# The second half of a modulation row: products on TensorE in four groups of 32 columns in place of multiply-adds on VectorE

## The chip, the cores and the metric

The kernel runs on one core of a Trainium2 chip. The metric is the device time of one execution in microseconds, the median of several. The engines of the core run their own instruction streams in order: TensorE (PE, with its weight loads shown apart as PEld), VectorE (DVE), ScalarE (ACT), GpSimd (POOL) and SyncE (SP), which issues most of the DMA transfers.

## The reference

One layer of a diffusion backbone: 1024 latent and 256 context tokens of width 1024. A modulated norm feeds one input projection, three mixers (LRU, RWKV-7, S5), a gated sum, and a gated SwiGLU block. What the change touches is the modulation, whose six pieces of 1024 columns come from one vector-matrix product with `w_mod` (1024 x 6144, 32 bit):

```python
cond_lat = jax.nn.silu(c)
m_lat = (cond_lat @ w_mod[i] + b_mod[i])[:, None, :]
sh1l, sc1l, gt1l, sh2l, sc2l, gt2l = jnp.split(m_lat, 6, axis=-1)
...
z_lat = modulate(rms_norm(h_lat, norm1[i]), sh1l, sc1l) @ w_in[i]
ys_l, zg_l, _ = token_mixers(z_lat, lp, st_lru, st_rwkv, st_s5, rows)
h_lat = h_lat + gt1l * merge_project(ys_l, zg_l, w_branch[i], w_out[i])
h_lat = h_lat + gt2l * swiglu(modulate(rms_norm(h_lat, norm2[i]), sh2l, sc2l), w_ffn_in[i], w_ffn_out[i])
return rms_norm(h_lat, norm_f)
```

The first two pieces (`sh1`, `sc1`) are needed at once. The other four (4096 columns: both gates, and the second shift and scale) are needed only after the mixers.

## The kernel before, in words

The large products go through "split" parts: each 32-bit operand is a high part `xh`, `wh` and a rest `xl`, `wl`, and three products (`xh,wh`, `xl,wh`, `xh,wl`) make one 128x512 tile in a PSUM bank `mm`. Small results use four other PSUM banks, `aux`, in turn.

The program's order is: `front` (first norm; the first 2048 columns of the modulation by `modrow`, which already places four products of 32 output columns side by side on TensorE); `s5_u` for q = 0 to 3 and `s5_front` for q = 0 to 3 (transposes L442, products L453 and L467, copies L477 into the state `s5h`); `s5_scan`, which POOL executes as 34 steps of four instructions (L498 to L501); four LRU tiles (convolution L137 and L140 on VectorE, gates and scans L161 to L173 on VectorE, `gi` and `ya` L176 and L181 on POOL); `s5_carry` for e = 0 to 7 (L522, L523 on VectorE and POOL); `s5_back` for e = 0 to 7 (L562 and after); then `s5_out`, RWKV and the FFN.

Three kinds of background work are laid between these. The gates of the branches, `zg` (products L1311 on tiles `zh`, `zl`), come in pieces of three products, and `fill` takes some pieces after each step. The input projections (`inproj`, L1305) belong to the steps. The third is the generator `mod2`, which makes the other 4096 columns: 16 blocks of 256 columns, and for each block four pieces, of two 128-row parts of `w_mod` each, so 64 pieces. Four pieces are taken after each `s5_u` and each `s5_front`, and 11 after each of the LRU tiles 0 to 2:

```python
for q in range(4):
    s.s5_front(q, s5g)
    mix(mod2, 4, FF)
...
for j in range(4):
    s.lru_tile(j, lp)
    if j < 3:
        side(mod2, 11)
    s.fill(FL)
for e in range(8):
    s.s5_carry(e, m2)
```

`cs` holds silu(c), one column for each 128 rows. The load of a piece, `wm2` in the code and `wm` in the trace (256 KB, two buffers), is issued by SP as soon as its buffer is free. In that same ring of two buffers, "wm2", the carry's temporaries `s5ct` are placed later. The instructions of each engine are put into their order by a scheduler with a timeline of its own, so that a changed piece also moves its neighbours.

## Time and profile before

| what | value |
|---|---|
| median of three runs | 2371.12 us (2370.62 to 2376.17) |
| profiled execution, its span | 2372.2 us |
| TensorE busy over the span | 2103.7 us (89%) |
| VectorE busy | 1729.6 us (73%) |
| POOL busy | 1176.5 us (50%) |
| all `mod2` work on VectorE, 78 to 496 us | 96.6 us |

The profiled execution's own time is the span; its instructions begin and end with it. Busy shares over the whole span are averages over stages with different limits, so the stages up to 640 us are shown separately below. A 32-bit product shows as two records in the trace, a product of split parts as one.

### The profile page before, as it was taken

To read this page: it belongs to the slowest core of one execution; us is meant where nothing else is said; L and a number is where in the kernel's file an instruction comes from. 1 tells how busy PE (TensorE), PEld (TensorE's weight loads), DVE (VectorE), ACT (ScalarE), POOL (GpSimd) and SP (SyncE) were. 2 spreads that over 40 slices of the span, in tenths; PEclk is the share of its full clock that TensorE was granted. 3 is DMA by queue.
4 is the path that set the end of the run, shared out by engine and by line. 5 is a ranking of instruction groups with operands and counts; after the bars stand their busy time and mean duration, and the time that the engine had idled before them with its cause. 6 is when DMAs were issued, how large, how long until landed. Compare 5 with 4: busy or idle time off the path is not lost.

```text
span 2372.2 us, 38912 instructions
## 1 busy us (share of the span) xinstructions
PE 2103.7 (89%) x14441; PEld 1663.8 (70%) x14441; DVE 1729.6 (73%) x2435; ACT 930.5 (39%) x1791; POOL 1176.5 (50%) x1283
## 2 busy tenths in 40 slices
PE   5989978887999988987799999897999999978888
PEld 3868766665888777866576676685888888755666
DVE  5556688988657878899833368738856666699998
ACT  5313344532435545554434234344332333233333
POOL 3651489955323576774000133535645454467664
PEclk8989998998999989997799999998999999989889
DMA  6634322223743444546868676632433232353333
GB/s 250 167 108 120 84 69 86 78 80 75 172 134 108 137 133 123 152 126 180 222 164 191 158 206 163 217 109 91 129 89 111 89 111 89 119 177 107 114 115 123
DMA packets 404379, 313.05 MB, mean 132 GB/s; under 512 B 67608, under 2 KB 369887, under 8 KB 403167
## 3 DMA queue, kind: packets, MB, share of 16 engines
q1 hardware_dynamic: 400606, 299.04, 44.7%
q10 hardware_dynamic: 2880, 10.49, 1.2%
q8 instruction: 114, 1.87, 0.4%
q0 software_dynamic: 704, 1.05, 0.2%
q14 instruction: 75, 0.61, 0.1%
HBM read 216.15 MB, written 94.35 MB: 131 GB/s over the span
## 4 chain that ended last, share of the span: by engine, by line
PE 46%; DVE 24%; POOL 10%; DMA 9%; issue 7%; ACT 3%; SPq 1%; DVEq 0%; POOLq 0%; ACTq 0%
PE mm L1565 17%; PE mm L1305 7%; PE mm L1311 7%; DVE hh L1479 3%; PE cg L1011 2%; DVE wt L1479 2%; PE mm L1735 2%; PE cu L998 2%; PE cg L985 2%; DMA wm<-in_w_mod_dram 2%; DMA hraw<-hidd 1%; PE cy L1026 1%; POOL s L214 1%; POOL nt L911 1%; DVE macc L1271 1%
## 5 line engine op out<-in xcount | busy, mean ns | idle before, releaser
L1565 PE MATMUL mm<-q,wt 128*128 128x512 f32 x1584 | 376.7, 398 | 4.5 <-DVE q L1479 3.5
L1565 PEld LDWEIGHTS mm<-q,wt 128*128 128x128 f32 x1584 | 299.6, 189 | 77.5 <-DVE q L1479 4.0
L1735 PE MATMUL mm<-wt,hh 128*128 128x512 f32 x924 | 248.9, 427 | 52.3 <-DVE wt L1479 12.1
L1735 PEld LDWEIGHTS mm<-wt,hh 128*128 128x128 f32 x924 | 184.5, 204 | 116.5 <-DVE wt L1479 18.1
L1305 PE MATMUL mm<-xh,wh 128*128 128x512 f32 (+1 forms) x576 | 215.0, 381 | 9.4 <-ACT ya L180 7.2
L1305 PE MATMUL mm<-xl,wh 128*128 128x512 f32 (+1 forms) x576 | 214.7, 380 | 1.2 <-DVE xl L1221 1.2
L1311 PE MATMUL mm<-xh,zh 128*128 128x512 f32 x384 | 160.4, 418 | 7.9 <-ACT zge L1347 5.1
L1311 PE MATMUL mm<-xl,zh 128*128 128x512 f32 x384 | 159.0, 414 | 0.0
L1305 PE MATMUL mm<-xh,wl 128*128 128x512 f32 (+1 forms) x576 | 139.9, 380 | 9.3 <-DVE wl L1298 7.0
L1478 ACT ACTIVATE wt<-wT 128x512 fp32r<-128x512 f32 x132 | 81.5, 628 | 160.6 <-PE mm L1565 129.0
L1479 DVE TENSOR_TENSOR wt<-wT,wt 128x512 fp32r<-128x512 f32 x132 | 135.7, 1035 | 2.6 <-ACT wt L1478 1.7
L1305 PEld LDWEIGHTS mm<-xh,wh 128*128 128x128 f32 x576 | 114.2, 198 | 29.8 <-ACT ya L180 8.0
L1305 PEld LDWEIGHTS mm<-xl,wh 128*128 128x128 f32 x576 | 113.8, 198 | 19.5 <-DVE xl L1221 1.5
L1311 PE MATMUL mm<-byt,bwh 128*128 128x512 f32 x384 | 118.7, 428 | 7.9 <-ACT bwh L1297 2.5
L1479 DVE TENSOR_TENSOR hh<-hraw,hh 128x256 fp32r<-128x256 f32 (+1 forms) x132 | 119.1, 925 | 8.6 <-ACT hh L1478 8.6
L1311 PE MATMUL mm<-xh,zl 128*128 128x512 f32 x384 | 110.7, 425 | 16.2 <-DVE zl L1298 16.2
L1305 PEld LDWEIGHTS mm<-xh,wl 128*128 128x128 f32 x576 | 102.1, 195 | 30.0 <-DVE wl L1298 8.7
L1015 DVE TENSOR_TENSOR x<-cg,pcend 64x256 f32<-64x256 f32 x152 | 63.9, 421 | 78.6 <-PE cg L1011 36.1
L1295 POOL CAST bwh<-bwr 128x512 fp32r<-128x512 f32 x16 | 10.0, 624 | 209.2 <-PE mm L1311 111.6
L1478 ACT ACTIVATE hh<-hraw 128x256 fp32r<-128x256 f32 (+1 forms) x132 | 56.2, 447 | 145.4 <-DMA hraw<-hidd 121.0
L1271 DVE SCALAR_TENSOR_TENSOR macc<-wm,cs,macc 128x256 f32<-128x256 f32 x112 | 87.6, 782 | 24.5 <-DMA wm<-in_w_mod_dram 22.2
L1311 PEld LDWEIGHTS mm<-xh,zl 128*128 128x128 f32 x384 | 76.2, 203 | 36.2 <-DVE zl L1298 18.7
(437 smaller groups left out, 5081.8 us busy)
## 6 DMA issues: line engine op xcount, KB each, us to landing
wt<-in_w_ffn_in_dram SPq DMA_DIRECT2D x44, 512.0 KB
hidd<-ft SPq DMA_DIRECT2D x75, 256.0 KB
wm<-in_w_mod_dram SPq DMA_DIRECT2D x64, 256.0 KB
gyl<-gyl SPq DMA_DIRECT2D x32, 512.0 KB
wr<-in_w_in_dram SPq DMA_DIRECT2D x27, 512.0 KB
zr<-in_w_in_dram SPq DMA_DIRECT2D x24, 512.0 KB
sgd<-zge SPq DMA_DIRECT2D x48, 256.0 KB
bsg<-sgd SPq DMA_DIRECT2D x48, 256.0 KB
```

Of the source, the lines that this page charges most:

```text
L214: G.tensor_tensor(o, a, b, op=op)
L985: s.pe = nc.tensor.matmul(ps[32 * q : 32 * q + 32, 64 * p : 64 * p + 64], gy[:, 2 * p + par, c - cb, 0:32], st["x"][:, p, par, :], start=T ...
L998: s.pe = nc.tensor.matmul(ps[o : o + 32, 64 * p : 64 * p + 64], st["tt"][32 * q : 32 * q + 32, p, st["cc"], :], st["gs"][32 * q : 32 * q + ...
L1011: s.pe = nc.tensor.matmul(sn[64 * par : 64 * par + 64, 64 * p : 64 * p + 64], sd[:, st["cc"], 2 * p + par, :], st["x"][:, p, par, :], star ...
L1015: V.tensor_tensor(xn[0:64, :, par, :], sn[r].rearrange("p (a k) -> p a k", a=4), vb(s.pcend[r, d, :, st["c"]], 64), op=ALU.mult)
L1271: nc.vector.scalar_tensor_tensor(acc, wm[:, j], s.cs[:, k + j, 0:1], acc, op0=ALU.mult, op1=ALU.add)
L1305: s.nc.tensor.matmul(ps, w(k), a(k), start=n == 0, stop=n == len(seq) - 1)
L1311: s.nc.tensor.matmul(ps, w[:, k], a[:, k], start=n == 0, stop=n == len(seq) - 1)
L1478: s.nc.scalar.activation(hi, raw, AF.Copy)
L1479: (eng or s.nc.vector).tensor_tensor(lo, raw, hi, op=ALU.subtract)
L1565: nc.tensor.matmul(ps, w[:, k], a[:, k], start=n == 0, stop=n == len(seq) - 1)
L1735: nc.tensor.matmul(ps, hid[k][c][h], w[k][name][b], start=start and n == 0, stop=stop and n == len(seq) - 1)
```

## The change

`mod2` keeps its 64 pieces, their loads and their places in the program. In a piece, TensorE takes a column of `cs`, broadcast to 32 columns, as stationary operand, and a stretch of 64 columns of the piece as moving operand; four such products (m = 0 to 3) go to partitions 0, 32, 64 and 96 of one `aux` bank, and the two row parts (j) add up there. VectorE then copies (first piece of a block) or adds (others) the 128x64 result to the accumulator `macc`. At the block's end one transpose of `macc` and two small copies take the place of two products with a column of ones and one copy. The gate rows `gtr` go from the ring of `macc` to the ring "wm2". The diff's other hunks take away descriptions and comments, and lines behind them shift by two (L1305 becomes L1307, L1311 becomes L1313).

```diff
     def mod2(s, pool):
-        ones = pool.tile([P, 1], F32, name="ones", tag="ones")
-        nc.gpsimd.memset(ones, 1.0)
         s.mod2t = md = s.cp.tile([P, 4, 8], F32, name="mod2t", tag="mod2t")
         mp = md.rearrange("p c k -> p (c k)")
         W = D // 4
         for c in range(16):
-            acc = pool.tile([P, W], F32, name="macc", tag="macc")
+            acc = pool.tile([P, 64], F32, name="macc", tag="macc")
             for k in range(0, KD, 2):
                 wm = pool.tile([P, 2, W], F32, name="wm2", tag="wm2", bufs=2)
                 src = s.i["w_mod"][0][P * k : P * k + 2 * P, 2 * D + W * c : 2 * D + W * c + W]
                 nc.sync.dma_start(wm, src.rearrange("(k p) c -> p k c", p=P))
+                ps = s.aux()
                 for j in range(2):
-                    if k + j == 0:
-                        nc.vector.tensor_scalar(acc, wm[:, j], s.cs[:, 0, 0:1], None, op0=ALU.mult)
-                    else:
-                        nc.vector.scalar_tensor_tensor(acc, wm[:, j], s.cs[:, k + j, 0:1], acc, op0=ALU.mult, op1=ALU.add)
+                    for m in range(4):
+                        nc.tensor.matmul(ps[32 * m : 32 * m + 32, 0:64], s.cs[:, k + j, 0:1].to_broadcast([P, 32]), wm[:, j, 64 * m : 64 * m + 64],
+                                         start=j == 0, stop=j == 1)
+                if k == 0:
+                    nc.vector.tensor_copy(acc, ps[:, 0:64])
+                else:
+                    nc.vector.tensor_tensor(acc, acc, ps[:, 0:64], op=ALU.add)
                 yield
             ps = s.aux()
+            nc.tensor.transpose(ps[0:64, 0:P], acc, s.ident)
             for m in range(2):
-                nc.tensor.matmul(ps[:, m : m + 1], acc[:, P * m : P * m + P], ones, start=True, stop=True)
-            nc.vector.tensor_copy(mp[:, 2 * c : 2 * c + 2], ps[:, 0:2])
+                nc.vector.tensor_copy(mp[64 * m : 64 * m + 64, 2 * c : 2 * c + 2], ps[0:64, 32 * m : 32 * m + 65 : 64])
         nc.vector.tensor_tensor(mp, mp, s.pv("b_mod")[:, 16:48], op=ALU.add)
         nc.vector.tensor_scalar(md[:, 2], md[:, 2], 1.0, None, op0=ALU.add)
         nc.vector.tensor_tensor(md[:, 2], md[:, 2], s.pv("norm2"), op=ALU.mult)
         for j, c in enumerate((0, 3)):
             ps = s.aux()
             nc.tensor.transpose(ps[:8, :P], md[:, c], s.ident)
-            t = pool.tile([8, P], F32, name="gtr", tag="macc")
+            t = pool.tile([8, P], F32, name="gtr", tag="wm2", bufs=2)
             nc.vector.tensor_copy(t, ps[:8, :P])
             nc.sync.dma_start(s.gt_d[j], t)
```

TensorE, between the third and the fourth `s5_front` (L467 the third's last products, L442 the fourth's first transposes; `xh,wh` and the like are input projections, `xh,zh` and the like gates), before:

```order
L467 MATMUL aux<-s5u,s5wb 128x160 x5
L1311 MATMUL mm<-xh,zh 128x512
L1311 MATMUL mm<-xl,zh 128x512
L1275 MATMUL aux<-ones,macc 128x1 x2
L1305 MATMUL mm<-xh,wh 128x256
L1305 MATMUL mm<-xl,wh 128x256
L1305 MATMUL mm<-xh,wh 128x256
L1305 MATMUL mm<-xl,wh 128x256
L1305 MATMUL mm<-xh,wh 128x256
L442 MATMUL aux<-ident,s5wt 128x128 x4
```

and with the change, the same place:

```order
L467 MATMUL aux<-s5u,s5wb 128x160 x5
L1268 MATMUL aux<-wm_2167,cs 32x64 x8
L1307 MATMUL mm<-xh,wl 128x512 x3
L1268 MATMUL aux<-wm_2200,cs 32x64 x8
L1307 MATMUL mm<-xh,wl 128x512 x4
L1313 MATMUL mm<-xh,zh 128x512
L1313 MATMUL mm<-xl,zh 128x512
L1313 MATMUL mm<-xh,zh 128x512
L1313 MATMUL mm<-xl,zh 128x512
L1313 MATMUL mm<-xh,zl 128x512 x8
L1268 MATMUL aux<-wm_2231,cs 32x64 x8
L1307 MATMUL mm<-xh,wh 128x512
```

The two ones-products are gone; groups of eight small products stand between the background products, and more of the latter (seven further rows follow) come ahead of L442.

VectorE around the convolution of LRU tile 1 (L137 and L140), before:

```order
L137 TENSOR_SCALAR xc<-xap,pv_1305 128x256
L140 SCALAR_TENSOR_TENSOR xc<-xap,pv_1305,xc 128x256
L1276 COPY mod2t<-aux 128x2
L1269 TENSOR_SCALAR macc<-wm_3212,cs 128x256
L140 SCALAR_TENSOR_TENSOR xc<-xap,pv_1305,xc 128x256
L1271 SCALAR_TENSOR_TENSOR macc<-wm_3212,cs,macc 128x256
L140 SCALAR_TENSOR_TENSOR xc<-xap,pv_1305,xc 128x256
L1271 SCALAR_TENSOR_TENSOR macc<-wm_3216,cs,macc 128x256 x2
L1271 SCALAR_TENSOR_TENSOR macc<-wm_3220,cs,macc 128x256 x2
L1271 SCALAR_TENSOR_TENSOR macc<-wm_3224,cs,macc 128x256
L1298 TENSOR_TENSOR wl<-wr,wh 128x1024
L1271 SCALAR_TENSOR_TENSOR macc<-wm_3224,cs,macc 128x256
```

and with the change:

```order
L137 TENSOR_SCALAR xc<-xap,pv_1439 128x256
L1300 TENSOR_TENSOR wl<-wr,wh 128x1024
L140 SCALAR_TENSOR_TENSOR xc<-xap,pv_1439,xc 128x256
L1273 TENSOR_TENSOR macc<-macc,aux 128x64
L137 TENSOR_SCALAR xc<-xap,pv_1439 128x1024
L140 SCALAR_TENSOR_TENSOR xc<-xap,pv_1439,xc 128x256
L140 SCALAR_TENSOR_TENSOR xc<-xap,pv_1439,xc 128x1024
L140 SCALAR_TENSOR_TENSOR xc<-xap,pv_1439,xc 128x256
L1273 TENSOR_TENSOR macc<-macc,aux 128x64
L140 SCALAR_TENSOR_TENSOR xc<-xap,pv_1439,xc 128x1024 x2
L1278 COPY mod2t<-aux 64x2 x2
```

The multiply-adds that stood one by one between the convolution's instructions are now few additions of 128x64, and the convolution's wide instructions come with its narrow ones.

VectorE at the start of the carry (L522 and L523), before:

```order
L1271 SCALAR_TENSOR_TENSOR macc<-wm_3618,cs,macc 128x256 x2
L1298 TENSOR_TENSOR wl<-wr,wh 128x1024
L522 TENSOR_TENSOR s5ct<-s_32_865,s5h 128x496
L522 TENSOR_TENSOR s5ct<-s_33_866,s5h 128x496
L137 TENSOR_SCALAR xc<-xap,pv_1305 128x1024
L523 TENSOR_TENSOR s5h<-s5h,s5ct 128x4x4x31
L1276 COPY mod2t<-aux 128x2
L140 SCALAR_TENSOR_TENSOR xc<-xap,pv_1305,xc 128x1024
L523 TENSOR_TENSOR s5h<-s5h,s5ct 128x4x4x31
L1277 TENSOR_TENSOR mod2t<-mod2t,pv_209 128x32
L522 TENSOR_TENSOR s5ct<-s_32_865,s5h 128x496
```

and with the change:

```order
L1278 COPY mod2t<-aux 64x2 x2
L1279 TENSOR_TENSOR mod2t<-mod2t,pv_209 128x32
L1280 TENSOR_SCALAR mod2t<-mod2t 128x8
L1281 TENSOR_TENSOR mod2t<-mod2t,pv_209 128x8
L1300 TENSOR_TENSOR wl<-wr,wh 128x1024
L1286 COPY gtr<-aux 8x128 x2
L522 TENSOR_TENSOR s5ct<-s_32_865,s5h 128x496
L522 TENSOR_TENSOR s5ct<-s_33_866,s5h 128x496
L523 TENSOR_TENSOR s5h<-s5h,s5ct 128x4x4x31 x2
L522 TENSOR_TENSOR s5ct<-s_32_865,s5h 128x496
L522 TENSOR_TENSOR s5ct<-s_33_866,s5h 128x496
```

Before, the convolution of tile 3 (L137, L140) and the end of `mod2` alternate with the carry; with the change they stand ahead of it, the copies of `gtr` included.

## Rows read from the trace of the kernel before

**Rows 1.** The page's first line.

```profile
span 2372.2 us, 38912 instructions
```

**Rows 2.** Busy time by stage: stretch (us), its length, then busy us of each engine (instructions), granted clock, DMA.

```profile
75.00:277.00 202.00, 189.88 (x986) 160.12 (x985) 116.92 (x269) 59.69 (x102) 87.74 (x202) 0.94 0.47 127
277.00:493.00 216.00, 173.21 (x688) 131.04 (x687) 192.54 (x159) 94.21 (x111) 199.23 (x166) 0.91 0.28 84
493.00:583.00 90.00, 75.27 (x289) 57.83 (x288) 78.55 (x79) 35.45 (x42) 42.23 (x20) 0.89 0.18 59
583.00:640.00 57.00, 49.39 (x319) 45.15 (x318) 36.03 (x46) 19.42 (x21) 23.56 (x21) 0.94 0.71 147
```

**Rows 3.** The chain of waits, 60 to 600 us, shares by line.

```profile
by line: issue 6.6%; PE mm L1311 5.3%; DMA wm<-in_w_mod_dram 4.7%; POOL s L214 4.5%; DVE macc L1271 4.5%; DVE s5ct L522 3.8%; DVE xc L140 3.7%; POOL s5ct L522 3.4%; POOL s5p L499 3.3%; DVE zl L1298 3.2%; PE mm L1305 3.2%; POOL s L233 3.1%; 
```

**Rows 4.** Busy time by stage of instructions on `macc` alone.

```profile
75.00:277.00 202.00, 4.27 (x32) 4.65 (x32) 34.59 (x68) 0.94 0.47 127
277.00:493.00 216.00, 4.74 (x28) 4.70 (x28) 62.04 (x60) 0.91 0.28 84
```

**Rows 5.** Tile `macc`, 75 to 277 us: min/median/max ns; below, VectorE's idle us, times.

```profile
L1271 DVE SCALAR_TENSOR_TENSOR macc<-wm,cs,macc x59: 447/485/1239, 78.5 to 277.0; 128x256 f32<-128x256 f32 x59
...
  DMA wm<-in_w_mod_dram: 17.5, 12
```

**Rows 6.** Tile `macc`, 277 to 500 us, the same lines.

```profile
L1271 DVE SCALAR_TENSOR_TENSOR macc<-wm,cs,macc x54: 453/1080/2554, 277.0 to 493.5; 128x256 f32<-128x256 f32 x54
...
  DMA wm<-in_w_mod_dram: 6.5, 7
```

**Rows 7.** Timeline of TensorE, 268 to 274 us: start, us, instruction.

```profile
271.28 1.52 PE L467 MATMUL aux<-s5u,s5wb 128*128 128x160 f32 x10
```

**Rows 8.** Timeline of POOL, 270 to 300 us.

```profile
276.62 1.23 POOL L498 TENSOR_TENSOR s5p<-s5h,s 128x320 f32<-128x320 f32 x1 [0.36 <-DVE s5h L477]
...
293.71 0.93 POOL L498 TENSOR_TENSOR s5p<-s5h,s 128x320 f32<-128x320 f32 x1
...
297.70 0.95 POOL L498 TENSOR_TENSOR s5p<-s5h,s 128x320 f32<-128x320 f32 x1
```

**Rows 9.** Line L86, small copies out of PSUM: min/median/max ns.

```profile
L86 DVE COPY pv<-aux x3: 175/225/241, 3.0 to 133.7; 128x16 f32<-128x16 f32 x1, 128x64 f32<-128x64 f32 x1, 128x87 f32<-128x87 f32 x1
```

**Rows 10.** Timeline of TensorE, 9 to 20 us, a step of `modrow`.

```profile
13.32 1.06 PE L1193 MATMUL aux<-wm,cw 128*32 128x512 f32 x8
```

**Rows 11.** Timeline of TensorE, 198 to 208 us.

```profile
202.30 1.03 PE L442 MATMUL aux<-ident,s5wt 128*128 128x128 f32 x8
203.17 3.66 PE L453 MATMUL aux<-s,s5wt 128*128 128x32 f32 x32
```

**Rows 12.** Timeline of the weight loads, 12.5 to 14 us.

```profile
13.31 0.16 PEld L1193 LDWEIGHTS aux<-wm,cw 128*32 128x32 f32 x8 [0.17 <-issue]
```

**Rows 13.** Timeline of TensorE, 122 to 125 us.

```profile
123.00 0.39 PE L1311 MATMUL mm<-xh,zh 128*128 128x512 f32 x1
123.22 0.39 PE L1311 MATMUL mm<-xl,zh 128*128 128x512 f32 x1
```

**Rows 14.** Timeline of TensorE, 131 to 136 us.

```profile
131.93 0.76 PE L1275 MATMUL aux<-ones,macc 128*128 128x1 f32 x4 [3.31 <-DVE macc L1271]
```

**Rows 15.** Timeline of POOL, 330 to 352 us.

```profile
334.62 2.46 POOL L176 TENSOR_TENSOR gi<-gi 128x1024 f32<-128x1024 f32 x1 [5.80 <-DVE gi L173]
...
346.05 1.00 POOL L498 TENSOR_TENSOR s5p<-s5h,s 128x320 f32<-128x320 f32 x1
...
350.43 1.00 POOL L498 TENSOR_TENSOR s5p<-s5h,s 128x320 f32<-128x320 f32 x1
```

**Rows 16.** Timeline of POOL, 470 to 497 us.

```profile
474.95 3.56 POOL L176 TENSOR_TENSOR gi<-gi 128x1024 f32<-128x1024 f32 x1 [3.67 <-DVE gi L173]
...
492.81 0.43 POOL L501 TENSOR_TENSOR s5h<-s5h,s5p 128x64 f32<-128x64 f32 x1
```

**Rows 17.** Timeline of VectorE, 488 to 505 us.

```profile
498.38 1.27 DVE L140 SCALAR_TENSOR_TENSOR xc<-xap,pv,xc 128x1024 f32<-128x1024 f32 x1
```

## The prediction

> **What bounds the kernel now.** I began with the top of the page: the profiled execution spans 2372.2 us [rows 1], 1.1 us over the median of the three timed runs (2371.12), so a sum made against the span is lowered by 1.1 at its end. All of `mod2` runs before 500 us, and the program's order is the same again from `s5_out` on, so I cut that part into four stages and read the busy time of each engine in each [rows 2]. Stage A (75 to 277 us, up to the start of POOL's scan) is TensorE's: 189.88 of 202 us busy, VectorE 116.92. Stage B (277 to 493, scan and LRU tiles) is POOL's, 199.23 of 216, with VectorE close behind at 192.54. Stage C (493 to 583, the carry) shows VectorE at 78.55 of 90, and stage D (583 to 640, `s5_back`) TensorE at 49.39 of 57. The chain of waits over 60 to 600 us agrees that nothing bounds all of it: its largest shares by line are 6.6, 5.3 and 4.7% [rows 3]. So the change has to be priced stage by stage.
>
> Next I took `macc` alone: VectorE spends 34.59 us on it in A and 62.04 us in B [rows 4], 96.6 us in all. The same instruction has a median of 485 ns in A [rows 5] and 1080 ns in B [rows 6]. Its idle time says what it waits for: in A the load of `wm`, 17.5 us in 12 waits; in B 6.5 us in 7. Today these waits stand on VectorE, which in A has room.
>
> The border of A and B is fixed by the last `s5_front` product on TensorE (271.28 for 1.52 us [rows 7]), after which VectorE's copy releases the scan on POOL at 276.62 [rows 8]. A later last product moves everything behind it.
>
> **The change part by part.** *What goes:* 128 multiply-adds, 96.6 us of VectorE [rows 4], and 64 ones-products in the trace, whose work the 16 transposes replace about evenly (9.0 us of TensorE now, by the same rows). *What comes on VectorE:* 64 copies or additions out of PSUM, 128x64. The nearest row, small copies out of PSUM, has 175 to 241 ns [rows 9]; at 0.2 us that is 13 us. 32 copies of 64x2 stand in place of 16 of 128x2, 3 us more. Net about -80 us of VectorE.
>
> *What comes on TensorE:* 64 groups of eight small products. A 32-bit product leaves two records, so a group is 16 records of 64 columns. No row shows one, but `modrow` uses the same placement in four column groups: 8 records of 512 columns take 1.06 us [rows 10]. Plain records of 128 columns cost 0.87/8 = 0.109 us (eight from 202.30 to 203.17 [rows 11]). If four run side by side, 8 records are the streaming of two, 2 x 4 x 0.109 = 0.87 us, which leaves 0.19 fixed; serial they would take 3.5. The new group is then 16/4 x 0.5 x 0.109 = 0.22 us of streaming, 0.19 fixed and the 0.17 us that the weight loads paused ahead of it [rows 12]: 0.58 us, 37 us for 64. From below it is 0.22. From above, `L453`'s records of 32 columns still take 3.66/32 = 0.11 each [rows 11], so 16 x 0.11 = 1.75 us if nothing overlaps. I take 0.58, since that placement is the same [rows 10]. The Trainium skill (TensorEngine Tiling (Array Packing), Key Properties) says that changing the tiling mode drains TensorE; the 0.17 us pause agrees with something of the kind, and by the rule a second pause on leaving each group would make 0.75 us, an estimate, and 5 us more in A.
>
> *Stage A.* The order of the two programs shows 29 groups ahead of the last `s5_front` product, and 47 background products (12 of the gates, 35 of the input projections) that stood behind it before. A background product starts 0.22 to 0.23 us after the one before [rows 13]. So +47 x 0.227 = 10.7 and +29 x 0.58 = 16.8, together 27.5 us. Against this stands TensorE's idle time in A, 12.1 us [rows 2]. The one wait of 3.31 us for `macc` [rows 14] goes, since its product goes; of the other 8.8 I take half, 4.4, as waits on VectorE that come sooner. A is then +27.5 - 7.7 = **+20**. Bounds: all idle time filled and groups at 0.22 give 10.7 + 6.4 - 12.1 = +5; none filled and the 17.5 us of `wm` waits [rows 5] now on TensorE give +45. The hiding place of the groups is only those 12 us; TensorE has no other cover here.
>
> *Stage B.* POOL waits twice for VectorE in the LRU tiles, 5.80 us [rows 15] and 3.67 us [rows 16], each time for a chain of long instructions on VectorE, among which the multiply-adds of B are laid. With 62.04 us of those gone from VectorE's queue [rows 4] the chain ends sooner by more than the wait, so I let both go: -9.5. Scan steps run at 297.70 - 293.71 = 4.0 us alone [rows 8] and at 350.43 - 346.05 = 4.4 us beside multiply-adds [rows 15]; 62.04 us of these make some 14 steps, 14 x 0.4 = 5.6. So B is **-15**, 201 us. TensorE must fit too: 173.21 + 35 x 0.58 + 23 further moved products (70 by the start of `s5_back` against 47) x 0.227 = 199 us, so it just fits, and nothing covers it any more. Bounds: 0 where TensorE's late products take the place of those waits; -17, the 199 us of TensorE's own work without a pause. The Trainium skill (SBUF — State Buffer, Who interferes with whom) says that a VectorE instruction with two SBUF inputs contends with a GpSimd instruction that reads SBUF, and one with at most one SBUF input does not. The 485 and 1080 ns agree on VectorE's side; by the rule alone POOL would win 60 x 0.485 = 29 us in place of 5.6, which the step of 4.4 us doesn't bear out.
>
> *Stage C.* In the order before, tile 3's convolution stands between the first carry steps; after, ahead of them, as VectorE is through with `mod2` sooner. Four instructions, 1.27 us one of them [rows 17], come to **-5**. Bounds: -9 with the last multiply-adds and the `wl` ahead of the carry counted (scan end 492.81 + 0.43 [rows 16]); +6 where the gate rows' transfers hold the two buffers of the ring "wm2", in which `gtr` now stands with the carry's temporaries: four waits at the 17.5/12 = 1.46 us of a load [rows 5].
>
> *Stage D.* 70 products (60 of 512 columns, 10 of 256) now stand ahead of `s5_back` that filled it before: 60 x 0.227 + 10 x 0.114 = 14.8 us. Part of them filled holes, so half: **-8** (0 to -15).
>
> *Queues.* SP issues the same 64 loads; its wait for a free buffer now ends with TensorE's products instead of VectorE's, so later background work on SP follows TensorE. POOL's order hardly changes.
>
> Sum: +20 - 15 - 5 - 8 = -8, 2364.2 against the span, **2363** against the median. A measurement of this kernel tells 0.3%, 7.1 us, from no change: faster is below 2364, slower above 2378.
>
> **The rivals.**
> (1) The forecast, 2353 to 2373.
> (2) VectorE is the true bound from 277 to 583: it is busy 271 of 306 us there [rows 2], and loses 53 net. TensorE then caps the gain: 173.21 + 75.27 + 26 = 274 of 306, so -32 in place of -20, and 20 - 32 - 8 = -20: 2351. For it speaks VectorE's 89%; against it, that a multiply-add's second half-microsecond in B is waiting, not work.
> (3) The other side: the waits for `wm` move from VectorE to TensorE, which takes its instructions in order, so that everything queued behind a group, `s5_front`'s products among it, waits too. 17.5 + 6.5 = 24 us [rows 5, 6]: -8 + 24 = +16, 2387. It decides from 15 us of such waits on. For it: two buffers, as before, and A is TensorE's. Against: a group holds a buffer for 0.58 us, two multiply-adds for 0.97, so that the loads run further ahead.
> (4) The column groups don't overlap: 1.75 us each, +34 in A alone, 2397; with B's 35 groups (61 us, so 173 + 61 + 5 = 239 us in place of 201) up to 2435. The row of `modrow` [rows 10] speaks against it, though its products are eight times as wide.
> (5) The change doesn't relieve POOL: TensorE, full in B, is late with the LRU tiles' projections, and B gains nothing. 20 - 5 - 8 = +7: 2378.
>
> **How the numbers follow.** Chances: (1) 0.40, (2) 0.20, (3) 0.20, (4) 0.06, (5) 0.14. The forecast's own spread lies over the lower limit of 0.3%: of its 0.40 I count 0.21 faster, 0.16 the same, 0.03 slower. (2) is faster, (3) and (4) slower, (5) half the same, half slower. Faster 0.41, same 0.23, slower 0.36. The range goes from 2345, under (2) for a well filled stage A, to 2388, over (3); (4) and the tails of (2) and (3) stay out. That is about 2 in 10.
>
> **What would show it.** A: the scan's first step at about 297 us and groups at 0.5 to 0.7 us; waits of TensorE for `wm` over 15 us in all mean (3), groups near 1.7 us mean (4). B: no waits of 4 to 6 us of POOL for `gi`, and some 201 us from the scan's first step to its last; 216 means (5), under 190 means (2). C: the carry starts without a convolution among its first steps. D: about 8 us shorter than 57. The forecast fails if stage A's idle time isn't filled, or if TensorE takes the place of POOL in B.

## The result, and the profile after

The changed kernel takes 2389.98 us (median of 4 runs, 2388.93 to 2392.62) against 2370.87 for the kernel before (4 runs): the ratio is 1.0076, with a 95% interval of 1.0058 to 1.0093. The interval lies above 1: by the ratio it is slower by 18 us, under 1%. 2363 was forecast, in a range of 2345 to 2388.

The first lines of the page of the changed kernel: span and busy time of each engine.

```profile
span 2390.8 us, 40867 instructions
...
PE 2127.8 (89%) x15417; PEld 1673.6 (70%) x15417; DVE 1643.5 (69%) x2387; ACT 928.6 (39%) x1791; POOL 1185.8 (50%) x1282
```

The answer to [rows 1]: the span is 18.6 us longer. VectorE is down to 1643.5 us from 1729.6, so 86 us left it, as forecast (80), and the time rose all the same.

The stages again, with the borders moved to where the events now lie (scan's start, scan's end, carry's end); columns as in [rows 2].

```profile
75.00:286.90 211.90, 203.61 (x1499) 166.04 (x1498) 87.21 (x241) 59.45 (x103) 83.05 (x199) 0.99 0.44 121
286.90:501.20 214.30, 179.24 (x1181) 131.62 (x1180) 142.50 (x143) 93.26 (x111) 204.97 (x166) 0.91 0.29 90
501.20:599.00 97.80, 86.67 (x355) 66.79 (x354) 73.53 (x74) 36.87 (x43) 41.59 (x18) 0.95 0.17 54
599.00:650.00 51.00, 31.72 (x220) 30.43 (x218) 38.53 (x46) 15.24 (x15) 24.75 (x17) 0.80 0.73 140
```

For comparison, the kernel before between the same events:

```profile
75.00:276.60 201.60, 189.48 (x984) 159.80 (x983) 116.52 (x268) 59.29 (x102) 87.35 (x201) 0.94 0.47 127
276.60:493.20 216.60, 173.81 (x691) 131.53 (x690) 193.14 (x159) 94.61 (x111) 199.81 (x166) 0.91 0.28 85
```

Stage A is 10.3 us longer and TensorE's idle time in it has shrunk from 12.1 to 8.3 us. Stage B is 2.3 us shorter, although VectorE is busy 142.5 us in it and not 193.1; POOL is busy 5 us *more*. The largest part of the loss lies in C. VectorE's timeline there, from the scan's end (501.17 us) on:

```profile
499.41 0.21 DVE L1273 TENSOR_TENSOR macc<-macc,aux 128x64 f32<-128x64 f32 x1
499.60 1.28 DVE L140 SCALAR_TENSOR_TENSOR xc<-xap,pv,xc 128x1024 f32<-128x1024 f32 x1
506.54 0.32 DVE L1278 COPY mod2t<-aux 64x2 f32<-64x2 f32 x2 [5.65 <-PE aux L1276]
506.89 0.19 DVE L1279 TENSOR_TENSOR mod2t<-mod2t,pv 128x32 f32<-128x32 f32 x1
...
510.73 1.22 DVE L1300 TENSOR_TENSOR wl<-wr,wh 128x1024 fp32r<-128x1024 f32 x1 [3.25 <-PE mm L1307]
511.88 0.47 DVE L1286 COPY gtr<-aux 8x128 f32<-8x128 f32 x2
516.55 1.94 DVE L522 TENSOR_TENSOR s5ct<-s,s5h 128x496 f32<-128x496 f32 x2 [4.21 <-DMA gtd<-gtr]
```

Before, the carry (L522) began 1.85 us after the scan's end at 493.24 [rows 16]:

```profile
495.09 1.98 DVE L522 TENSOR_TENSOR s5ct<-s,s5h 128x496 f32<-128x496 f32 x2
```

Now the scan has ended, the convolution is done at 500.88, and until 516.55 VectorE mostly waits: for a transpose of `macc` (5.65 us), for the buffer of a weight part, which background products on TensorE still read (3.25), and then for the store of the gate rows (4.21, `DMA gtd<-gtr`). The chain of waits over 485 to 530 us shows why that transpose is late (start, us, what):

```profile
489.40 2.31 POOL ya L181
...
491.82 0.25 SPq L182
...
492.12 0.02 SPq L1264
...
492.16 3.74 DMA wm<-in_w_mod_dram
...
496.04 1.33 PE aux L1268 x32
497.37 9.02 PE mm L1307 x30
```

POOL ends `ya` of LRU tile 2, SP stores it (L182) and only then comes to the last two loads of `wm` (L1264); the groups wait for these, and the transpose that closes the block stands behind 30 background products on TensorE (9.02 us). While TensorE waited 5.70 us for these loads its granted clock fell to 0.50, the lower of its two levels (1.2 of 2.4 GHz), where it stayed from 495 to 501.5 us; the first ten of the 30 products came 0.43 us apart and not 0.23, which is some 2 us of the 9.02. Before, VectorE got its sums at once, as it made them itself.

Events of both kernels, and of the experiments below, read from the traces (first start and last end of the scan L498 to L501, of the carry L522/L523, and of the products of `s5_back`; us from the first instruction). "Rest" goes from there to the last instruction. Its program is the same in all, but the scheduler has moved up to 48 of its 11,900 TensorE records across the border; in the changed kernel 30 background products, some 7 us, are missing from it.

| kernel | scan | its length | carry begins after | carry | s5_back's products | rest | time, ratio to before |
|---|---|---|---|---|---|---|---|
| before | 276.62 to 493.24 | 216.6 | 1.85 | 495.09 to 582.96 | 589.94 to 634.20 | 1735.0 | 2370.87 |
| changed | 286.94 to 501.17 | 214.2 | 15.38 | 516.55 to 599.45 | 605.81 to 649.46 | 1738.3 | 2389.98, 1.0076 |
| 1 own tile | 288.90 to 501.03 | 212.1 | 0.03 | 501.06 to 586.11 | 592.99 to 641.18 | 1731.8 | 2377.35, 1.0018 |
| 2 before, ring | 272.93 to 489.74 | 216.8 | 12.72 | 502.46 to 587.28 | 591.63 to 637.40 | 1737.6 | 2385.15, 1.0051 |
| 3 VectorE, then TensorE | 270.63 to 482.20 | 211.6 | 11.18 | 493.38 to 582.13 | 587.79 to 634.28 | 1729.8 | 2373.78, 1.0001 |
| 4 TensorE, then VectorE | 289.05 to 508.78 | 219.7 | 0.03 | 508.81 to 593.54 | 599.83 to 642.67 | 1741.2 | 2388.68, 1.0060 |
| 5 half left out | 273.78 to 485.65 | 211.9 | 0.03 | 485.68 to 574.08 | 580.45 to 628.68 | 1736.6 | 2367.72, 0.9983 |
| 6 groups doubled | 299.95 to 513.25 | 213.3 | 12.55 | 525.80 to 613.65 | 620.03 to 663.78 | 1734.7 | 2398.87, 1.0110 |
| 7 mixed, 16/17/0 | 271.51 to 462.36 | 190.9 | 0.03 | 462.39 to 548.90 | 588.19 to 632.86 | 1730.7 | 2374.39, 1.0011 |
| 8 before, 16/17/0 | 272.50 to 471.80 | 199.3 | 1.26 | 473.06 to 567.09 | 586.94 to 631.43 | 1735.8 | 2374.14, 1.0015 |
| 9 mixed, 12/13/8 | 273.38 to 478.05 | 204.7 | 0.04 | 478.09 to 573.33 | 582.22 to 624.72 | 1733.4 | 2362.86, 0.9966 |
| 10 all left out | 265.83 to 478.85 | 213.0 | 0.03 | 478.89 to 568.22 | 572.46 to 619.72 | 1731.8 | 2356.92, 0.9931 |
| 11 before, 12/13/8 | 274.37 to 491.88 | 217.5 | 1.27 | 493.15 to 581.00 | 587.37 to 632.05 | 1734.3 | 2370.19, 0.9992 |
| 12 own tile, 12/13/8 | 285.62 to 486.17 | 200.6 | 9.56 | 495.73 to 584.72 | 590.40 to 636.13 | 1726.5 | 2367.71, 0.9990 |

The time of each is the median of its runs, the ratio is to runs of the kernel before on the same chip. The events are those of one profiled execution, which need not be a middle one: it was the fastest of its kernel in experiments 2 and 7 (2379.92 and 2368.61 us). "Rest" spreads over 15 us, with a granted clock between 0.943 and 0.952. And experiment 3, whose TensorE has the same instructions in the same order as before up to the last `s5_front` product, starts the scan 6.0 us earlier. Its stage A, in the columns of the windows above:

```profile
75.00:270.60 195.60, 183.63 (x996) 155.17 (x995) 117.17 (x267) 58.88 (x101) 87.38 (x201) 0.97 0.48 131
```

Idle 12.0 us as before (12.1), but a granted clock of 0.97 and not 0.94. A difference of a few us between two single profiles is therefore worth little, and several profiles tell more. TensorE's order up to the last `s5_front` product is that of the kernel before in eight of them (before, 2, 3, 5, 7, 8, 9, 11): the scan starts at 270.6 to 276.6 us, at 273.2 in the mean, and the kernel before is the latest. It is that of the changed kernel in four (changed, 1, 4, 12): 285.6 to 289.1, 287.6 in the mean. So the change costs stage A some 14 us, not the 10.3 of the first two profiles. The scan's length is 216.6 to 217.5 us with multiply-adds in stage B (before, 2, 11), 211.6 to 214.2 with products on TensorE (changed, 1, 3, 6) and 211.9 to 213.0 with neither (5, 10). In experiments 7, 8, 9 and 12 only two LRU tiles' `gi` and `ya`, not three, lie within the scan, so their lengths do not compare with these.

### The profile page after: what moved, and what is told of

It is laid out like the page before. It is cut to its first block, busy times and chain, and to the rows that moved or that the text cites. A ratio compares the mean times of both kernels' runs of the same rounds, so it can differ in the third digit from the quotient of the medians.

```text
span 2390.8 us, 40867 instructions
## 1 busy us (share of the span) xinstructions
PE 2127.8 (89%) x15417; PEld 1673.6 (70%) x15417; DVE 1643.5 (69%) x2387; ACT 928.6 (39%) x1791; POOL 1185.8 (50%) x1282
## 4 chain that ended last, share of the span: by engine, by line
PE 50%; DVE 21%; POOL 9%; DMA 8%; issue 7%; ACT 4%; SPq 1%; DVEq 0%; POOLq 0%; ACTq 0%
PE mm L1567 17%; PE mm L1307 10%; PE mm L1313 8%; PE cg L1011 3%; DVE hh L1481 2%; DVE wt L1481 2%; PE mm L1737 2%; PE cg L985 2%; PE cu L998 2%; POOL s L214 2%; DMA hraw<-hidd 2%; PE cy L1026 1%; DVE rn L748 1%; PE aux L609 1%; PE aux L843 1%
## 5 line engine op out<-in xcount | busy, mean ns | idle before, releaser
L1307 PE MATMUL mm<-xh,wh 128*128 128x512 f32 (+1 forms) x576 | 218.1, 387 | 23.5 <-ACT wh L1299 13.0
L1307 PE MATMUL mm<-xl,wh 128*128 128x512 f32 (+1 forms) x576 | 217.3, 385 | 1.2 <-DVE xl L1221 1.2
L1313 PE MATMUL mm<-xh,zh 128*128 128x512 f32 x384 | 158.7, 413 | 9.2 <-ACT zge L1349 5.1
L1313 PE MATMUL mm<-xl,zh 128*128 128x512 f32 x384 | 156.5, 408 | 0.0
L1307 PEld LDWEIGHTS mm<-xh,wh 128*128 128x128 f32 x576 | 114.9, 200 | 45.0 <-ACT wh L1299 13.8
L1307 PE MATMUL mm<-xh,wl 128*128 128x512 f32 (+1 forms) x576 | 138.1, 377 | 3.7 <-DVE wl L1300 2.5
L1307 PEld LDWEIGHTS mm<-xl,wh 128*128 128x128 f32 x576 | 114.5, 199 | 20.2 <-DVE xl L1221 1.5
L1313 PE MATMUL mm<-byt,bwh 128*128 128x512 f32 x384 | 118.9, 428 | 6.4 <-DVE bsg L1380 2.1
L1307 PEld LDWEIGHTS mm<-xh,wl 128*128 128x128 f32 x576 | 101.2, 193 | 24.2 <-DVE wl L1300 3.4
L1313 PE MATMUL mm<-xh,zl 128*128 128x512 f32 x384 | 105.8, 410 | 5.5 <-DVE zl L1300 5.5
L1002 ACT ACTIVATE x<-cu 32x256 f32<-32x256 f32 x156 | 58.5, 375 | 102.3 <-PE cu L998 99.3
L1481 DVE TENSOR_TENSOR wt<-wt 128x512 fp32r<-128x512 f32 x66 | 71.9, 1091 | 35.6 <-ACT wt L1480 35.6
```

The source lines that it names most:

```text
L1002: S.activation(st["x"][96:128, :, par, :], ps[o : o + 32, 0:256].rearrange("p (a k) -> p a k", a=4), AF.Copy)
L1307: s.nc.tensor.matmul(ps, w(k), a(k), start=n == 0, stop=n == len(seq) - 1)
L1313: s.nc.tensor.matmul(ps, w[:, k], a[:, k], start=n == 0, stop=n == len(seq) - 1)
L1481: (eng or s.nc.vector).tensor_tensor(lo, raw, hi, op=ALU.subtract)
```

## The experiments

**1. The gate rows in a tile of their own.** The ring "wm2" then holds the loads and the carry's temporaries alone, as in the kernel before.

```diff
+        tt = pool.tile([40, P], F32, name="gtr", tag="gtr")
         for j, c in enumerate((0, 3)):
...
-            t = pool.tile([8, P], F32, name="gtr", tag="wm2", bufs=2)
+            t = tt[32 * j : 32 * j + 8]
```

> The changed kernel with the two gate rows in a tile of their own instead of in the ring of the loads and of the carry's temporaries. Theory: the 15 us between the scan's end and the carry's start come from that ring, because the carry's first temporary has to wait for the last group, its transpose, the gate rows' transposes and their stores. Then the carry starts within 2 to 3 us of the scan's end, as it did before, and the time falls by 12 to 14 us to about 2376. Rival: the carry is late because TensorE is late with the LRU tile's products; then the gap stays over 10 us and the time stays at 2388 to 2391.

Measured 2377.35 us, ratio 1.0018 (1.0005 to 1.0031). VectorE's timeline at the same place:

```profile
498.51 1.28 DVE L140 SCALAR_TENSOR_TENSOR xc<-xap,pv,xc 128x1024 f32<-128x1024 f32 x1
499.71 0.22 DVE L1273 TENSOR_TENSOR macc<-macc,aux 128x64 f32<-128x64 f32 x1
501.06 2.00 DVE L522 TENSOR_TENSOR s5ct<-s,s5h 128x496 f32<-128x496 f32 x2 [1.14 <-POOL s5h L501]
502.98 1.28 DVE L140 SCALAR_TENSOR_TENSOR xc<-xap,pv,xc 128x1024 f32<-128x1024 f32 x1
504.16 0.23 DVE L1273 TENSOR_TENSOR macc<-macc,aux 128x64 f32<-128x64 f32 x1
```

The carry waits only for POOL's last scan instruction (L501), and the rest of the convolution and the last additions (L1273) lie behind its start. The gap of 15.38 us is gone, and by the ratios (1.0076 against 1.0018) some 14 of the 18 us of loss with it. The theory holds for the gap: it was the ring. In the profiles the end of `s5_back`'s products comes 8.3 us earlier; 6.5 us more lie in the rest, where the granted clock is 0.950 here and 0.943 in the changed kernel, and why that is so is not shown.

**2. The ring alone, in the kernel before.**

```diff
-            t = pool.tile([8, P], F32, name="gtr", tag="macc")
+            t = pool.tile([8, P], F32, name="gtr", tag="wm2", bufs=2)
```

> The kernel before with only the ring of the gate rows changed as the change does it. Theory of the ring: the carry has to wait for the end of the modulation here too, but that end is reached sooner since the multiply-adds stay on VectorE; a gap of 6 to 15 us at the carry's start and 2376 to 2386. Rival (the ring costs nothing by itself): 2371.

Measured 2385.15 us, ratio 1.0051 (1.0034 to 1.0068). One changed tag, no product added:

```profile
500.80 0.48 DVE L1284 COPY gtr<-aux 8x128 f32<-8x128 f32 x2 [3.31 <-PE aux L1282]
502.46 2.06 DVE L522 TENSOR_TENSOR s5ct<-s,s5h 128x496 f32<-128x496 f32 x2 [1.18 <-DMA gtd<-gtr]
```

The carry starts 12.72 us after the scan and waits for the end of the same way, the gate rows' transpose (`<-PE aux L1282`, 3.31) and their store. The line of the change that looks least, a tag, costs two thirds of the whole by itself (0.51 of 0.76%).

**3 and 4. Half of the blocks in each form**, gate rows in the accumulator's ring as before (both in one tile); 3 has `te = c >= 8`, 4 has `te = c < 8`.

```diff
         for c in range(16):
+            te = c >= 8
...
+                if te:
+                    ps = s.aux()
...
+                else:
                     for j in range(2):
...
```

> Blocks 0 to 7 by multiply-adds on VectorE, blocks 8 to 15 by products on TensorE, gate rows in the ring of the accumulator as before. Theory: the 10 us by which the scan starts later come from the groups and the moved products of stage A, so that here the scan starts at 275 to 278 us as before; stage B gains the 2 to 3 us it gained, and the whole is 2366 to 2370. Rival (the later scan start is not due to these groups, or multiply-adds were what held POOL up in stage B): the first would give 2376, the second under 2360.

> The reverse: blocks 0 to 7 by products on TensorE, blocks 8 to 15 by multiply-adds on VectorE, gate rows in the ring of the accumulator as before. Theory: the scan starts 10 us late as in the changed kernel, stage B takes 216 us as before, the carry starts at once: 2379 to 2382. Rival (stage B is what lost): 2371.

Measured 2373.78 us, ratio 1.0001 (0.9988 to 1.0014), for experiment 3 and 2388.68, 1.0060 (1.0044 to 1.0076), for 4. The scan starts at 270.63 us where VectorE does the first half and at 289.05 us where TensorE does: stage A's delay belongs to its own groups and the background products that move ahead with them. The whole of 3 missed its forecast of 2366 to 2370 because its carry starts 11.18 us late, with the ring as before. TensorE's timeline, and then that of SP, show where:

```profile
482.84 1.36 PE L1273 MATMUL aux<-wm,cs 128*32 128x64 f32 x32 [12.50 <-DMA wm<-in_w_mod_dram]
484.12 0.80 PE L1324 MATMUL mm<-xl,wh 128*128 128x512 f32 x1
```

```profile
478.49 0.34 SPq L182 DMA_DIRECT2D yd<-ya  x1
478.92 5.69 SPq L1268 DMA_DIRECT2D wm<-in_w_mod_dram  x4
```

SP issued four loads (L1268 in this kernel) right behind the store of tile 2's `ya` (L182). TensorE, which takes its instructions in order, waited 12.5 us for them with the next LRU tile's products queued behind, and VectorE, with the carry behind in its queue, then waited 6.91 us for these. This is the rival (3) of the prediction, in one place. Experiment 4 came out 7 us above its forecast; its scan takes 219.7 us, and its rest is 6.2 us longer than before, at a granted clock of 0.943 against 0.948; which part of that is the mix is not known.

**5. Multiply-adds of blocks 8 to 15 left out**, in the kernel before.

```diff
-                    else:
+                    elif c < 8:
                         nc.vector.scalar_tensor_tensor(acc, wm[:, j], s.cs[:, k + j, 0:1], acc, ...)
```

> The kernel before, in which blocks 8 to 15 leave out all multiply-adds but their first instruction (so the gates and the second modulation lack part of their sum); loads, ones-products and copies stay. About 53 us of VectorE go from stage B and nothing comes to TensorE. Theory (POOL's own work and the LRU tiles' long VectorE instructions set stage B, the multiply-adds were hidden): the scan takes 209 to 214 us against 216.6, and the time falls by 2 to 8 us only. Rival (multiply-adds held POOL up, and TensorE's new groups ate the gain in the changed kernel): 200 us or less, a time under 2357.

Measured 2367.72 us, ratio 0.9983 (0.9971 to 0.9994). Busy times from scan's start to its end:

```profile
273.78:485.65 211.87, 175.75 (x715) 135.35 (x714) 141.31 (x111) 96.51 (x115) 200.27 (x166) 0.91 0.27 84
```

VectorE is busy 141.3 us instead of 193.1, and POOL's 200.27 is no less than before. With nothing in their place, the multiply-adds of stage B are worth 4.7 us of scan length and 4 us of time. The forecast had put 15 on them.

**6. Every group's products made twice**, in the kernel of experiment 1. The second pass starts the sums over, so the modulation is not doubled as the expectation says.

```diff
-                for j in range(2):
+                for j in (0, 1, 0, 1):
```

> The changed kernel with the gate rows in a tile of their own, and each group's products made twice over (the second pass adds the same sums again, so the modulation is twice too large). If a group costs 0.40 us of TensorE, as the 12.3 us of 496 records ahead of the scan say, and TensorE has no idle time left there, the scan starts 10 to 13 us later than at 288.9 us, and the time is 2385 to 2395. Rival (the groups lie in holes of TensorE, and the moved background products alone made the scan late): the start moves by under 4 us.

Measured 2398.87 us, ratio 1.0110 (1.0093 to 1.0126); the scan starts at 299.95 us, 11.05 later than in experiment 1. The groups' line by TensorE, ahead of the scan, in the changed kernel and here (busy us, mean ns of a record, idle before):

```profile
L1268 PE MATMUL aux<-wm,cs 128*32 128x64 f32 x496 | 12.3, 224 | 2.7 <-issue 2.4
```

```profile
L1268 PE MATMUL aux<-wm,cs 128*32 128x64 f32 x992 | 19.0, 224 | 7.2 <-DMA wm<-in_w_mod_dram 4.4 <-issue 2.8
```

12.3 us for 31 groups are 0.40 us for each, and the second pass of 496 records adds 6.7 us, 0.22 us for each group. So a group is 0.22 of streaming and 0.18 fixed. The other 4.5 us of the 11 are idle time ahead of groups, mostly waits for `wm` (4.4 us, none before): there is no room left in TensorE's stage A. That split is rough, as the granted clock of the stage is 0.95 here and 0.98 in experiment 1. Later TensorE waited 13.15 us for the last loads, behind tile 2's store as in experiment 3, so the time rose by more than the 11 us.

**7 and 8. The last pieces earlier**: 16 and 17 after LRU tiles 0 and 1, none after tile 2; 7 on the kernel of experiment 3, 8 on the kernel before.

```diff
-            if j < 3:
-                side(mod2, 11)
+            if j < 2:
+                side(mod2, 16 + j)
```

> Blocks 0 to 7 on VectorE, 8 to 15 on TensorE as in the third experiment, and the last 33 pieces taken after LRU tiles 0 and 1 (16 and 17) and none after tile 2. There TensorE had waited 12.5 us for a load that SP could issue only behind the store of tile 2's output, and the carry began 11 us late. Theory: with the loads ahead of that store the carry starts within 3 us of the scan's end, and the time is 2356 to 2364, below both kernels. Rival (the late carry is hidden elsewhere, or the wait moves to tile 1's store): 2367 or more.

> The kernel before with its last pieces taken in the same way after tiles 0 and 1 only, all by multiply-adds. Its carry starts 1.9 us after the scan already, so that nothing is to be gained there; what the multiply-adds delay in tile 1 is to be lost. 2371 to 2378. It tells whether a gain of the run before this one comes from the place of the pieces alone.

Measured 2374.39 us, ratio 1.0011 (0.9999 to 1.0023), and 2374.14, 1.0015 (1.0006 to 1.0024). Experiment 7 failed, and shows something: its scan ends at 462.36 and its carry at 548.90, 34 us earlier than before, and `s5_back` starts at 588.19 us, 1.8 us earlier. POOL's timeline of it:

```profile
514.61 3.02 POOL L176 TENSOR_TENSOR gi<-gi 128x1024 f32<-128x1024 f32 x1 [12.68 <-DVE gi L173]
...
572.88 3.23 POOL L176 TENSOR_TENSOR gi<-gi 128x1024 f32<-128x1024 f32 x1 [23.98 <-DVE gi L173]
576.19 2.90 POOL L181 TENSOR_TENSOR ya<-ya,gi 128x1024 f32<-128x1024 f32 x1
```

The scan and the carry ran ahead of LRU tile 2, whose `gi` (L176) came at 514.61 and not at 474.95 [rows 16], and the last tile ended at 579.1 us, 10 us later than in the kernel before (568.75). Behind the store of the last `ya` SP issues the loads of `s5_back`, and with one of these the chain of waits over 440 to 595 us ends (start, us, what):

```profile
583.36 7.77 DMA s5tz<-kkd
```

The second bound of this region is the chain of the four LRU tiles and the store behind it; an early carry is worth nothing when it pushes a tile back.

**9. The same mix, 12, 13 and 8 pieces.**

```diff
-                side(mod2, 11)
+                side(mod2, (12, 13, 8)[j])
```

> As the third experiment (blocks 0 to 7 on VectorE, 8 to 15 on TensorE), with the last 33 pieces taken 12, 13 and 8 after LRU tiles 0, 1 and 2, so that all loads stand ahead of the store of tile 2's output on SP. In the seventh experiment the carry ran ahead of tile 2 and nothing was won, because the LRU tiles ended as late as ever. Theory: here the carry starts within 3 us of the scan's end and the tiles keep their times, so that s5_back starts 8 to 11 us earlier than at 587.8 us and the time is 2358 to 2366. Rival (s5_back waits for the last LRU tile and not for the carry): s5_back starts at 585 to 590 us and the time is 2367 to 2375.

Measured 2362.86 us, ratio 0.9966 (0.9954 to 0.9978): the only version with the whole computation that beats the kernel before with its interval wholly below 1. Its carry waits for POOL's scan alone:

```profile
474.80 0.22 DVE L1278 TENSOR_TENSOR macc<-macc,aux 128x64 f32<-128x64 f32 x1 [0.85 <-PE aux L1273]
478.09 1.08 DVE L522 TENSOR_TENSOR s5ct<-s,s5h 128x496 f32<-128x496 f32 x1 [3.07 <-POOL s5h L501]
```

`s5_back` starts at 582.22 us, 7.7 earlier than before and 5.6 earlier than in experiment 3, where 8 to 11 were expected. One thing is not taken apart: the granted clock over the whole execution has a mean of 0.943 in these six runs and of 0.9395 in the eleven runs of the kernel before on the same chip, and 0.0035 of 2371 us is 8 us, as much as the gain. Whether the clock is higher because waits have gone, or for another reason, no run shows.

**10. All but the first two of the eight instructions of each block left out**, in the kernel before.

```diff
-                    else:
+                    elif k + j == 1:
```

> The kernel before, in which every block leaves out all multiply-adds but its first two instructions (k = 0 and 1), in stage A as well as in B; loads, ones-products and copies stay. It shows the most that taking the multiply-adds from VectorE can give when nothing comes to TensorE. Theory (they were hidden nearly everywhere): 2360 to 2368, with the scan's start 2 to 6 us earlier than in the kernel before and its length 210 to 214 us. Rival (they cost what the forecast had): 2350 or less.

Measured 2356.92 us, ratio 0.9931 (0.9914 to 0.9949): taking three quarters of them away for nothing gives 14 to 16 us, more than the theory, which had 2360 at the least. It is 10.8 us less than experiment 5, and the scan starts 10.8 us earlier than before (at the same granted clock of 0.94) and 7.4 earlier than the mean of the eight, at a length of 213; 2 to 6 us earlier were expected. So the multiply-adds were not hidden in stage A, though VectorE has room there. TensorE's idle time in it is 7.1 us and not 12.1: its wait of 3.3 us for `macc` is gone, and those for VectorE's `zl` are 5.3 us and not 7.0. Some 15 us for three quarters of the work is the sum from which any price on TensorE has to be paid.

**11 and 12. The place of the pieces by itself**: the step of experiment 9 on the kernel before, and on that of experiment 1.

> The kernel before, all multiply-adds, with its pieces taken 12, 13 and 8 after tiles 0, 1 and 2 as in the ninth experiment. If that run's gain comes from the mix (VectorE in stage A, TensorE in stage B): 2368 to 2375 here. If it comes from the place of the pieces alone: 2360 to 2365.

> All blocks by products on TensorE, gate rows in a tile of their own, and the pieces taken 12, 13 and 8. Theory: the 12 us by which the groups and the moved products start the scan late in stage A remain, so 2372 to 2378 against the mix's 2363. Rival (with the end in order, TensorE's form is as good in stage A): 2360 to 2366.

Measured 2370.19 us, ratio 0.9992 (0.9982 to 1.0003), and 2367.71, 0.9990 (0.9980 to 1.0000). With the multiply-adds the place does nothing. With products everywhere it brings the changed kernel's form level with the kernel before, under the theory's 2372 to 2378 and over the rival's 2360 to 2366, though its scan starts 12 us later than in experiment 9 and its carry 9.56 us after the scan. That gap is not the ring's: the scan has run ahead of LRU tile 2, and the carry stands on VectorE behind this tile's scans and a weight part. The mix keeps 5 us over it.

## Why the prediction was wrong

The forecast had -8 and the profiles have +18.5. That miss of 26.5 us is 13.5 in C, 12.6 in B, 6.8 in D and 3.3 in the rest, less 9.7 in A, which came out cheaper than forecast. The step that failed most is stage C, "-5", with its upper bound "+6 where the gate rows' transfers hold the two buffers of the ring". The convolution did move ahead, and the carry itself got shorter by 5.0 us (87.87 to 82.89), the number forecast; as single profiles of the carry spread from 82.9 to 95.2 us, this may be chance. But the ring was priced as four waits of a load's length. What stands ahead of a buffer's release is the whole way to it: last load, last group, transpose, bias, second transpose, copy, store. In the changed kernel that way ends 15.38 us after the scan; before, the carry began after 1.85. Experiments 1 and 2 show it from both sides: some 14 us less without the ring, 12 us more with the ring alone, by the ratios. Without the ring the kernel is still not faster (1.0018); the forecast gain of B and D is what is missing there.

By the terms, from the table: A +10.3, B -2.4, the carry's late start +13.5, the carry itself -5.0, from its end to the first product of `s5_back` -0.6, `s5_back` -0.6, rest +3.3: +18.5.

- *The group.* 0.58 us was the estimate, 0.40 is measured (experiment 6): the streaming of 0.22 and the fixed 0.19 were right, the pause of 0.17 on top of them is not seen. That the products of four column groups overlap holds; rival (4) is out.
- *Stage A, +20.* Measured +10.3 in the two profiles, some 14 over all. The counts came out (29 groups, 47 products), and the work nearly: TensorE's busy time times its granted clock is 189.48 x 0.94 = 178 us before and 203.61 x 0.99 = 202 us after, 24 us more where 27.5 were forecast. The idle time gave 3.8, not the 7.7 taken. Two waits of the kernel before went (the first two lines), but others came, the largest ahead of groups (the third line, of the changed kernel):

```profile
PE mm L1311 <- DVE zl L1298: 7.0, 2, 5.1
PE aux L1275 <- DVE macc L1271: 3.3, 1, 3.3
PE aux L1268 <- issue: 2.4, 2, 1.8
```

The other 10 us are the clock, 0.99 in place of 0.94, which the forecast held constant; that A came out under its +20 is in good part luck. Against experiment 3 with its 0.97, stage A of the changed kernel is 16.3 us longer.
- *Stage B, -15.* Measured -2.4. POOL's waits for `gi` went as forecast:

```profile
POOL gi L176 <- DVE gi L173: 2.3, 1, 2.3
```

against 9.5 us [rows 15, 16]. But POOL's instructions took 205.0 us instead of 199.8. The term of 0.4 us for each of 14 scan steps was the wrong one: experiment 5 finds POOL at 200.3 us without any multiply-add beside it. In a row the steps beside multiply-adds are 4.4 and not 4.0 us; in the sum this does not come back. That the steps beside the LRU tiles' long instructions on VectorE now carry the difference is argued, not shown. By the Trainium skill (SBUF — State Buffer, Who interferes with whom) a VectorE instruction with two SBUF inputs contends with a GpSimd instruction that reads SBUF; the prediction worked that out to 29 us, an estimate, and POOL's busy time in experiment 5 (200.3 us against 199.8) shows none of it.
- *Stage D, -8.* Measured -0.6 for `s5_back`'s products and -0.6 for the way to the first of them. Of the 70 background products that moved ahead, only 40 are gone from between `s5_back`'s (64 before, 24 now), the other 30 from the rest. From the first to the last of its products TensorE is busy 31.3 us and not 39.2, but idle 12.4 and not 5.0, and its granted clock is 0.79 and not 0.92. Its timeline shows what the background products had filled:

```profile
605.81 1.31 PE L562 MATMUL aux<-s5h,s5wc 128*128 128x128 f32 x4 [6.51 <-DVE s5wc L552]
611.17 0.76 PE L563 MATMUL aux<-s5u,s5tz 128*128 128x128 f32 x2 [4.06 <-DMA s5u<-u]
...
631.04 0.97 PE L562 MATMUL aux<-s5h,s5wc 128*128 128x128 f32 x4 [3.09 <-DVE s5h L557]
636.53 0.77 PE L563 MATMUL aux<-s5u,s5tz 128*128 128x128 f32 x2 [4.51 <-DMA s5u<-u]
```

`s5_back` waits for loads of `u` (4.06 and 4.51 us) and for VectorE (6.51 ahead of its first product, 3.09 within); the 40 background products, some 9 us at 0.227 each, had cost nearly nothing there.

- *The rivals.* (3) named the nearest time, 2387, by another way: TensorE's waits for `wm` are 9.2 us in four in stage B, not 24, and the largest part of the loss lies at the carry, where VectorE waits for TensorE and the gate rows' store. (2), VectorE as the bound, falls with experiment 5. (5) is right in that B gains nearly nothing, but POOL and not TensorE is what keeps it so: with nothing on TensorE in place of the multiply-adds (experiment 5) the scan is as long as with products.

## What to carry to other kernels

Before work moves to an engine with a queue in order, follow its *last* piece to whoever needs the buffer that it holds: a shared ring makes the next user wait for the end of the whole chain, and here that one tag cost two thirds of the loss. Remove the suspected work for nothing first (experiments 5 and 10): its worth, some 4 us in stage B and 7 to 12 in stage A, was far from its busy time of 62 and 35 us, and in the opposite order. Then a mix by stage, VectorE where TensorE is full and TensorE where it has holes, with the last loads ahead of the store that blocks their queue, was faster than either pure form, by some 0.25%; what the clock has in that stays open.

## What the runs showed of the hardware

- TensorE's granted clock in stage A is 0.94 to 0.97 in the eight profiles of the same order, and 0.98 or 0.99 in the four of the changed one. In the kernel before it is 0.50 at 133 to 135 and 153 to 156 us, after single waits of 3.31 us for `macc` [rows 14] and 5.14 us for `zl`, at 170 to 176 us around two shorter waits (1.81 and 1.49), and at 208 to 210 and 256 to 261 us after products of 32 columns (L453). In the changed kernel the two long waits are gone, no wait in the stage is over 1.8 us, and the clock is 1.00 from 75 to 272 us. The total of the idle time does not tell it: experiment 10 has 0.94 with 7.1 us, 4.8 of them one wait. Nor does the order: in experiment 3 it is 1.00 from 208 us to the scan's start, and why is open. Over 200 us, 0.05 of it is 10 us, nearly as much as the change costs this stage.
- 16 records of 64 columns in four column groups took 0.40 us, and 16 more without leaving the group 0.22: 0.014 us a record, against 0.11 for the plain records of 32 columns [rows 11]. From the start of a group to the start of the next instruction it is 0.36 us.
- An addition of 128x64 with one operand in PSUM took 188 to 223 ns in all 48 cases of the changed kernel, those beside POOL's scan included (499.41 in the timeline above), where the multiply-add of 128x256 with both tensors in SBUF went from a median of 485 to one of 1080 ns [rows 5, 6].
